# A hybrid decoder layer on one core: the sample group's two score runs and its value sums in one PE run per pair of pages, one raw weight tile, and page turns and gathers at other steps

## The chip, the cores and the metric

The kernel runs on one core of one Trainium2 chip. The metric is the device time of one execution in microseconds (us), and the median of a few executions is compared. Beside these plain times there is one execution taken by the hardware profiler, from which every row quoted below comes. Engine names are those of the profile: PE is the matrix engine's matmuls and PEld its weight loads, DVE the vector engine, ACT the scalar engine, POOL GpSimd, and SP the engine whose queue issues most plain transfers.

## The reference

One decoder layer is computed for a prompt group (1 sequence of 2048 tokens) and for a sample group (8 sequences of 4 new tokens, each with 8192 earlier tokens in a paged cache of keys and values). Both go through the same projection into eleven groups of 512 columns, four mixers (convolution, pooling, stick-breaking attention, cross-attention to 256 memory tokens), gates, an output product and norms. The cut below keeps the projection, the memory product and the stick-breaking attention, which the change touches; the other mixers are as their names say.

```python
D_MODEL, SEQ, DEC_BATCH, DEC_SEQ, PAST_LEN, PAGE_SIZE = 1024, 2048, 8, 4, 8192, 128
SB_HEADS, SB_HEAD_DIM, MEM_HEADS, N_MEM, CONV_K, Q_BLOCK = 8, 64, 4, 256, 31, 128
SPLIT_SIZES = (512,) * 11          # ca cb cg pu pg q k v sg mq mg

def sb_block(q, k, v, bias, q_pos, k_pos):
    z = (jnp.einsum('nqhd,nkhd->nhqk', q, k).astype(jnp.float32) * (SB_HEAD_DIM ** -0.5)
         + bias.astype(jnp.float32)[None, :, None, None])
    mask = (k_pos[None, :] < q_pos[:, None])[None, None]
    log_beta = jax.nn.log_sigmoid(z)
    log_1m = jnp.where(mask, jax.nn.log_sigmoid(-z), 0.0)
    rc = lax.cumsum(log_1m, axis=3, reverse=True)
    a = jnp.exp(jnp.where(mask, log_beta + rc - log_1m, -jnp.inf))
    return jnp.einsum('nhqk,nkhd->nqhd', a.astype(v.dtype), v)

def mem_kv(mem, g, w):
    kv = rms_norm(mem, g) @ w
...

def mixer_layer(x, pos, conv_hist, pool_hist, sb_fn, mk, mv, pre_g, post_g, w_in, ...):
    h = rms_norm(x, pre_g)
    z = h @ w_in
    ca, cb, cg, pu, pg, q, k, v, sg, mq, mg = jnp.split(z, ...)
    y_c, conv_new = conv_branch(ca, cb, conv_hist, w_dw, b_dw, ln_g, ln_b, w_pw, b_pw)
    y_p, pool_new = pool_branch(pu, pool_hist, pos, pool_w, pool_scale)
    y_s = sb_fn(q, k, v, sb_bias).reshape(n, l, W_SB)
    y_m = mem_attend(mq.reshape(n, l, MEM_HEADS, MEM_HEAD_DIM), mk, mv).reshape(n, l, W_MEM)
    mix = jnp.concatenate([y_c * jax.nn.silu(cg), y_p * jax.nn.silu(pg),
                           y_s * jax.nn.silu(sg), y_m * jax.nn.silu(mg)], axis=-1)
    out = rms_norm(mix @ w_out, post_g)
    return x + out, conv_new, pool_new, k, v

# prompt group: sb_fn goes over its own 2048 keys in blocks of Q_BLOCK queries
# sample group: the keys are those of the cache, then its own four
k_past = cache_k[0][page_table].reshape(8, 8192, 8, 64)
v_past = cache_v[0][page_table].reshape(8, 8192, 8, 64)
y_s = sb_block(q, jnp.concatenate([k_past, k], axis=1),
               jnp.concatenate([v_past, v], axis=1), bias, pos_s, k_pos_s)
```

Outputs are both groups' results, the new keys and values, the last rows of convolution and pooling, and the memory keys and values. All is float32.

## The kernel before

**Order of work.** The kernel is one function written in a tile framework. PE's program order is the order of the code (a manual schedule for that engine). For the other engines a scheduler decides the order of the queue, and inserts the waits. Pools hand out tiles by a tag with a number of buffers; a tile of the tag can be written again when the last reader of the buffer's former content is done.

**Stages.** From 0 to about 1490 us the projection z = h @ w_in runs in two parts (1056 and 1024 tokens; column blocks of 384, 384, 288 and of 512, 512), with the product of the 256 memory tokens put between the first groups of part 0, and with convolution, pooling and cross-attention work beside it. The sample group's attention over the cache is interleaved with the projection's matmuls. From about 1490 to 2000 us follows the prompt's stick-breaking attention, then the output product and the norms to 2426.

**Projection weights.** A weight is 1024×128 float32 (512 KB), held as 128×8×128. `load_w` (L222) takes a raw tile "wr" with WR = 2 buffers and issues the load on SP's queue (L226). `split_w` (L229) makes two float32r tiles of it: hi, by ACT's cast (L232), and lo, by POOL's subtraction raw − hi (L233); "whi" and "wlo" have two buffers each. `mm3` (L236) multiplies with 24 matmuls: hi·xhi, hi·xlo, lo·xhi for each of 8 slices (L242). `fill_w` (L745) keeps up to two split weights and as many raw ones as WR allows. The order of the first weights is q0, q1, q2, mem0, mem1, mem2, q3, mem3, mem4, mem5, k0, mem6, mem7, k1, k2, k3, v0; "mem" are the eight weights of the memory product, each used for one block of 256 tokens, while a weight of the projection is used for all column blocks of its part. A group of the projection holds one weight or two (the names tell: z0mq, z0sg).

**Sample group.** The 64 pages of each of 8 sequences are handled in N = 64 steps, called pairs: two pages of four sequences at a time (two groups of 32 pairs). For each page, `load_k` gathers a key tile "kt" (128×2048, 1 MB; POOL issues an indirect DMA, L892), `turn` (L920) lays it into a tile "T" by two DVE transposes of 32×32 blocks (L925) and asks for the key tile of the next pair, and `scores` (L930) does 32 small matmuls into "sSA" (L938; the profile calls their shape 128*32). `load_v` gathers four value tiles "vt" (512 KB each). `weights` (L942) makes the attention weights of a pair: two ACT sigmoids, a DVE scan that goes on from the pair before (L955), a DVE product (L958). `transposes` (L961) turns them on PE and ACT copies them to "saT". `values` (L970) adds the pair's weighted values into "sO" with 16 matmuls (L977). `sample_setup` holds constants: the weights W of the scores, a small mask tile h8x, two tiles sgam.

The generator `sample_stages` is advanced one `yield` at a time by the projection's loop: at each unit of projection work `due` grows by a fixed rate times its cost, and whenever it is above 1 one step is run (L1803), so that the sample group's steps are spread over the projection. There are four steps per pair, and each puts what it holds between two units of projection matmuls:

- A: scores of page 0, then the turn of page 1
- B: transposes of the pair before
- C: scores of page 1, values of the pair before, all four value gathers, weights of this pair, the turn of page 0 of the next pair
- D: nothing

The tags and their buffers: "T" one (TB = 1, 8 KB per partition), "kt" two, "vt" four, "saT" two, "sbe" two.

Of the kernel before, what the change touches and what calls it, by code (L numbers as in the profile page):

```python
# [8 lines left out]
F32 = mybir.dt.float32  # L9
# [9 lines left out]
P = 128  # L19
# [13 lines left out]
PART = 1024  # L33
COLS = (((0, 384), (384, 768), (768, 1056)), ((0, 512), (512, 1024)))
XW = 1056
TB = 1
SMALL = 4
K4 = 4
PACE = 4.0
# [14 lines left out]
VB = 4  # L54
# [4 lines left out]
SEND = 0.97  # L59
XA = 3  # L60
KT = 2
WR = 2


class Tasks:
# [21 lines left out]
def kernel(  # L87
# [9 lines left out]
    pe, act, dve, pool, sp = nc.tensor, nc.scalar, nc.vector, nc.gpsimd, nc.sync  # L97
# [151 lines left out]
    st = zx.enter_context(tc.tile_pool(name="st", bufs=2, side="left"))  # L249
    tasks = Tasks()  # L250

    def big(name, bufs=BIG):
        return st.tile([P, 1088], F32, tag="big", name=name, bufs=bufs)

    def small(name):
        return st.tile([P, 512], F32, tag="small", name=name, bufs=SMALL)
# [488 lines left out]
    def fill_w(n=2):  # L745

        while len(wsplit) < n and (raw or SEQ_W):
# [3 lines left out]
            wsplit[it] = split_w(raw.pop(it), "%d%s%d" % it)  # L751
        while n == 2 and len(raw) < WR and SEQ_W:
            next_raw()
# [53 lines left out]
    def sample_setup(sm, S):  # L807

        ptb = sm.tile([P, NB, NPAGE], I32, tag="T", name="ptb", bufs=TB)
        sp.dma_start(ptb.rearrange("p b n -> p (b n)"), page_table.rearrange("b n -> (b n)").partition_broadcast(P))  # L810
# [55 lines left out]
                    dve.tensor_copy(W[pr, r, :, r, :, i], qv[pr, r, :, t0 : t0 + TS])  # L866
            S["W"].append(W.rearrange("p r j x q i -> p (r j) (x q i)"))

        h8 = sm.tile([P, 4, 2, 4], F32, name="h8x", bufs=1)
        pool.memset(h8, 1.0)  # L870
        pool.affine_select(out=h8, in_=h8, compare_op=ALU.is_ge, fill=0.0, base=0, pattern=[[-32, 4], [-4, 2], [-8, 4]],
                           channel_multiplier=1)
# [5 lines left out]
            dve.tensor_tensor(out=H8, in0=H8, in1=h8[:, i], op=ALU.add)  # L878
        S["H8"] = H8
        S["gam"] = []  # L880
        for k in range(2):
            g = sm.tile([P, 257], F32, name=f"sgam{k}", bufs=1)
            pool.memset(g[:, 256:257], 1.0)
            S["gam"].append(g)
        S["Oc"] = con.tile([P, 2, DH], F32, name="Oc")
        yield

# [6 lines left out]
    def sample_stages(sm, sps, S):  # L894
# [4 lines left out]
        N = 2 * NCK  # L899
        kts, vts, Ts, sSs, As, aTs = {}, {}, {}, {}, {}, {}  # L900
# [8 lines left out]
                gather(kt, krows, S["idk"][:, n // NCK, page(n, ml) : page(n, ml) + 1])  # L909
                kts[n, ml] = kt.rearrange("p (s j d) -> p s j d", s=4, d=32)  # L910

        def load_v(n):
            if n < N:
                vts[n] = []
                for i in range(4):
                    vt = sm.tile([P, 2 * 512], F32, tag="vt", name=f"vt{n}_{i}", bufs=VB)
                    gather(vt, vrows, S["idv"][:, 4 * (n // NCK) + i, page(n, 0) // 2 : page(n, 0) // 2 + 1])
                    vts[n].append(vt)

        def turn(n, ml):  # L920
            if n < N:
                T = sm.tile([P, 4, 16, 32], F32, tag="T", name=f"T{n}_{ml}", bufs=TB)
                kt = kts.pop((n, ml))
                for hh in range(2):
                    dve.transpose(T[:, 2 * hh : 2 * hh + 2].rearrange("p s j t -> p (s j t)"),  # L925
                                  kt[:, 2 * hh : 2 * hh + 2].rearrange("p s j d -> p (s j d)"))
                Ts[n, ml] = T
                load_k(n + 1, ml)
# [12 lines left out]

        def weights(n):  # L942
            sS = sSs.pop(n)
            be = sm.tile([P, 256], F32, tag="sbe", name=f"sbe{n}", bufs=2)
            ga = S["gam"][n % 2]

            tok = sS[:, :256].rearrange("p (m s t) -> p m t s", m=2, s=4)
            by = dict(m=2, s=4)
            act.activation(out=ga[:, 0:256].rearrange("p (m t s) -> p m t s", **by), in_=tok, func=AF.Sigmoid,
                           bias=S["nb1"][:, 0:1], scale=-1.0)  # L950
            act.activation(out=be.rearrange("p (m t s) -> p m t s", **by), in_=tok, func=AF.Sigmoid,
                           bias=S["b1"][:, 0:1])
            E = sm.tile([P, 257], F32, tag="sE", name=f"sE{n}", bufs=2)
            prev = S.get("E") if n % NCK else None
            dve.tensor_tensor_scan(out=E[:, ::-1], data0=ga[:, ::-1], data1=zeros.to_broadcast([P, 257]),  # L955
                                   initial=1.0 if prev is None else prev[:, 0:1], op0=ALU.mult, op1=ALU.max)
            S["E"] = E
            dve.tensor_tensor(out=be, in0=be, in1=E[:, 1:257], op=ALU.mult)  # L958
            As[n] = be

        def transposes(n):  # L961
            aps = S["ps"][:, 256:512]
            bs = As.pop(n).rearrange("p (k s) -> p s k", s=2)
            for k in range(2):
                pe.transpose(aps[:, P * k : P * (k + 1)], bs[:, k, :], ident)
            aT = sm.tile([P, 2, P], F32, tag="saT", name=f"saT{n}", bufs=2)
            act.copy(aT.rearrange("p l r -> p (l r)"), aps)
            aTs[n] = aT.rearrange("p l (x i) -> p l x i", i=4)

# [21 lines left out]
        for _ in range(Y0):  # L991
            yield
        turn(0, 0)
        for n in range(N):
            yield
            scores(n, 0)
            turn(n, 1)
            yield
            if n:
                transposes(n - 1)  # L1000
                yield

            scores(n, 1)
            if n:
                values(n - 1)
                load_v(n)
            weights(n)
            turn(n + 1, 0)
            yield
        yield  # L1010
        yield
        yield
        transposes(N - 1)
        yield
        yield
        values(N - 1)

# [759 lines left out]
    S = {}  # L1777
# [222 lines left out]
    for n, x in enumerate(parts):  # L2000
# [8 lines left out]
        prod, i, h = x  # L2009
# [5 lines left out]
        for k, p_ in enumerate(out_part(x) if n >= len(lead_) else lead if not n else ()):  # L2015
# [5 lines left out]
            if not n:  # L2021

                k, at_ = p_ % 4, p_ // 4
# [41 lines left out]
```

## Time and profile before

| what | value |
|---|---|
| time before, median of 3 runs | 2421.16 us (2418.48 to 2427.0) |
| profiled execution's span | 2426.4 us |
| mean granted clock of PE | 0.982 |
| HBM read / written | 469.28 MB / 90.68 MB, 231 GB/s over the span |
| key gathers: 128 issues, POOL busy | 125.6 us, 981 ns each |
| value gathers: 256 issues, POOL busy | 250.4 us, 978 ns each |
| page turns on DVE: 256 | 308.8 us, 1226 ns each |
| score matmuls: 4096, PE busy | 140.8 us |
| value matmuls: 1024, PE busy | 123.7 us |

Busy times are the time in which an engine has an instruction in work, over the whole span; a matmul's record overlaps the next one's, so for matmuls the distance between starts tells more than the duration. A row of the timeline gives the start, the duration, the engine, the line, the operation, output and inputs; the part in brackets is the idle time of the engine just before, and what ended it. Rows that begin with an engine and a tile and hold "<-" without a time are sums of waits: us in total, times, the longest.

### The profile page before, as it was taken

To read this page: it belongs to the slowest core of one execution; us is meant where nothing else is said; L and a number is where in the kernel's file an instruction comes from. 1 tells how busy PE (TensorE), PEld (TensorE's weight loads), DVE (VectorE), ACT (ScalarE), POOL (GpSimd) and SP (SyncE) were. 2 spreads that over 40 slices of the span, in tenths; PEclk is the share of its full clock that TensorE was granted. 3 is DMA by queue.
4 is the path that set the end of the run, shared out by engine and by line. 5 is a ranking of instruction groups with operands and counts; after the bars stand their busy time and mean duration, and the time that the engine had idled before them with its cause. 6 is when DMAs were issued, how large, how long until landed. Compare 5 with 4: busy or idle time off the path is not lost. (4 is left out here: it accounts for less than half of the span.)

```text
span 2426.4 us, 42151 instructions
## 1 busy us (share of the span) xinstructions
PE 2290.7 (94%) x15962; PEld 1776.1 (73%) x15962; DVE 1736.2 (72%) x2434; ACT 1118.5 (46%) x1939; POOL 1272.7 (52%) x1309
## 2 busy tenths in 40 slices
PE   6999999999999999999999999899999998989997
PEld 6998888898887777777777776455555556777775
DVE  5332784969756665477877877888898857886898
ACT  5322343242442322124241425688989955543444
POOL 2554545556574455655555554576876844433330
PEclk9999999999999999999999999999999999999998
DMA  5678988887778799987877776834332227887764
GB/s 184 213 253 285 350 290 292 290 263 265 261 253 275 271 346 329 312 285 253 290 265 271 260 239 164 239 81 118 101 88 73 63 63 239 272 279 254 238 240 161
DMA packets 340438, 562.15 MB, mean 232 GB/s; under 512 B 28481, under 2 KB 212929, under 8 KB 323834
## 3 DMA queue, kind: packets, MB, share of 16 engines
q1 hardware_dynamic: 284858, 290.72, 39.1%
q0 software_dynamic: 55376, 268.72, 31.1%
q8 instruction: 126, 2.06, 0.3%
q14 instruction: 78, 0.64, 0.1%
HBM read 469.28 MB, written 90.68 MB: 231 GB/s over the span
## 5 line engine op out<-in xcount | busy, mean ns | idle before, releaser
L925 DVE STREAM_TRANSPOSE T<-kt 128x1024 f32<-128x1024 f32 x256 | 308.8, 1226 | 193.6 <-PE sSA L938 183.0
L892 POOL DMA_INDIRECT vt<-in_cache_v_dram,idv x256 | 250.4, 978 | 239.7 <-PE sO L977 178.8
L583 DVE SCALAR_TENSOR_TENSOR cacc<-U,par,cacc 128x512 f32<-128x512 f32 x480 | 360.1, 750 | 11.8
L1277 POOL TENSOR_TENSOR be<-be,E 128x512 f32<-128x512 f32 (+2 forms) x320 | 303.5, 956 | 117.0 <-DVE E L1268 52.6
L1268 DVE TENSOR_TENSOR_SCAN E<-gam,cr,ZM 128x513 f32<-128x513 f32 x192 | 232.9, 1262 | 14.4 <-ACT gam L1253 13.2
L892 POOL DMA_INDIRECT kt<-in_cache_k_dram,idk x128 | 125.6, 981 | 206.9 <-DVE T L925 152.5
L1288 PEld LDWEIGHTS AT<-ident,be 128*128 128x128 f32 x1088 | 117.9, 142 | 127.3 <-ACT at L1294 45.3
L1885 PE MATMUL acc<-wohi,mh 128*128 128x512 f32 (+1 forms) x480 | 193.6, 403 | 3.9 <-DVE mh L1650 2.0
L1253 ACT ACTIVATE gam<-S,nbias_bc 128x1024 f32<-128x1024 f32 (+1 forms) x160 | 172.5, 1078 | 51.2 <-ACT be L1255 18.9
L1885 PE MATMUL acc<-wolo,mh 128*128 128x512 f32 (+1 forms) x480 | 190.8, 397 | 0.0
L1885 PE MATMUL acc<-wohi,ml 128*128 128x512 f32 x448 | 179.2, 400 | 12.1 <-DVE ml L1650 12.1
L1248 PE MATMUL S<-kT,Q 128*128 128x512 f32 (+1 forms) x640 | 177.9, 401 | 6.1 <-ACT be L1255 2.6
L1288 PE MATMUL AT<-ident,be 128*128 128x128 f32 x1088 | 158.4, 284 | 13.8 <-DVE at L1292 3.9
L1255 ACT ACTIVATE be<-S,bias_bc 128x1024 f32<-128x1024 f32 (+1 forms) x160 | 171.4, 1071 | 0.0
L1304 PE MATMUL av<-at,V 128*64 128x512 f32 (+3 forms) x640 | 153.0, 557 | 1.7 <-DVE sbo L1309 1.7
L938 PE MATMUL sSA<-T,W 128*32 128x128 f32 x4096 | 140.8, 277 | 7.6 <-DVE T L925 6.4
L938 PEld LDWEIGHTS sSA<-T,W 128*32 128x32 f32 x4096 | 105.4, 110 | 44.9 <-issue 37.2
L977 PE MATMUL sO<-vt,saT 128*32 128x512 f32 x1024 | 123.7, 597 | 0.0
L1248 PEld LDWEIGHTS S<-kT,Q 128*128 128x128 f32 x640 | 107.3, 196 | 22.2 <-ACT be L1255 3.5
L1650 DVE TENSOR_TENSOR ml<-mr,mh 128x512 fp32r<-128x512 f32 x108 | 97.0, 905 | 33.6 <-ACT mh L1639 33.4
L1265 DVE TENSOR_TENSOR_SCAN E<-gam,ZM 128x128 f32<-128x128 f32 (+3 forms) x128 | 96.4, 802 | 29.3 <-ACT gam L1253 22.3
L1294 ACT COPY at<-AT 128x512 f32<-128x512 f32 x192 | 109.0, 656 | 14.4 <-PE AT L1288 14.4
(571 smaller groups left out, 6032.8 us busy)
## 6 DMA issues: line engine op xcount, KB each, us to landing
Q<-qd SPq DMA_DIRECT2D x64, 256.0 KB
mr<-mixd SPq DMA_DIRECT2D x32, 512.0 KB
mr<-mixd SPq DMA_DIRECT2D x48, 256.0 KB
wor<-in_w_out_dram SPq DMA_DIRECT2D x20, 512.0 KB
xtp<-in_x_prompt_dram SPq DMA_DIRECT2D x16, 512.0 KB
kT<-kd SPq DMA_DIRECT2D x64, 128.0 KB
wor<-in_w_out_dram SPq DMA_DIRECT2D x32, 256.0 KB
msd<-mr SPq DMA_DIRECT2D x32, 256.0 KB
```

What stands on the lines that cost most here:

```text
L583: dve.scalar_tensor_tensor(out=ps, in0=U[:, a + k : a + k + H], scalar=wd[:, k : k + 1], in1=ps, op0=ALU.mult, op1=ALU.add)
L892: pool.indirect_dma_start(out=dst, out_offset=None, in_=rows, in_offset=bass.IndirectOffsetOnAxis(ap=idx, axis=0))
L925: dve.transpose(T[:, 2 * hh : 2 * hh + 2].rearrange("p s j t -> p (s j t)"), kt[:, 2 * hh : 2 * hh + 2].rearrange("p s j d -> p (s j d)"))
L938: pe.matmul(sSs[n][32 * g : 32 * g + 32, P * ml : P * (ml + 1)], lhsT=W[:, jj, :], rhs=T[:, :, jj, :], start=i == 0, stop=i == 3, tile_pos ...
L1248: pe.matmul(S[:, j, :w], lhsT=Q[hh][:, x, P * (q2 + j) : P * (q2 + j + 1)], rhs=KT[hp, hh, kc][:, :w], start=x == 0, stop=x == 1)
L1253: act.activation(out=ga[:, :, 512 - w : 512], in_=S[:, :, :w], func=AF.Sigmoid, bias=nbias_bc[:, h : h + 1], scale=-1.0)
L1255: act.activation(out=be[:, :, :w], in_=S[:, :, :w], func=AF.Sigmoid, bias=bias_bc[:, h : h + 1])
L1268: dve.tensor_tensor_scan(out=E[:, j][:, ::-1], data0=ga[:, j][:, ::-1], data1=ZM[:, 0:1].to_broadcast([P, 513]), initial=carry[hh, q2][:, ...
L1277: pool.tensor_tensor(out=be[:, j, :m], in0=be[:, j, :m], in1=E[:, j, 513 - w : 513 - w + m], op=ALU.mult)
L1288: pe.transpose(ap_[:, P * qt : P * (qt + 1)], A[hp, qb, kc, hh, qt][:, P * r : P * (r + 1)], ident)
L1304: pe.matmul(av[64 * hh : 64 * hh + 64, c], lhsT=V[:, 4 * kc + r, 64 * hh : 64 * hh + 64], rhs=ats.pop((hp, qb, kc, r, hh))[:, c], start=dg ...
L1885: pe.matmul(o[:rows], lhsT=m[a][:, k, :rows], rhs=W[prod, 4 * h + k][w], start=not cont and h == k == n == 0, stop=h == 1 and k == 3 and n ...
```

## The change

- A pair's scores of both pages and the value sums of the pair before become one step (A), and so one run on PE. The transposes of the pair's own weights come two steps later, in the same pair (C). Steps B and C take one page turn of the next pair each; step D holds nothing. The value gathers are written in two halves, two in A behind the value sums, two in B.
- Two T tiles in place of one; ahead of the first pair both its pages are turned, and two steps pass. At the end the last value sums come one step after the last pair.
- One raw weight tile in place of two. The tile "big" shrinks from 1088 to 1056 columns; h8x takes a buffer of the tag "vt"; sgam, sbe and saT have one buffer in place of two.

The arithmetic and the number of matmuls, turns, gathers and loads stay the same.

```diff
--- before.py
+++ after.py
@@ -33,7 +33,7 @@
 PART = 1024
 COLS = (((0, 384), (384, 768), (768, 1056)), ((0, 512), (512, 1024)))
 XW = 1056
-TB = 1
+TB = 2
 SMALL = 4
 K4 = 4
 PACE = 4.0
@@ -59,7 +59,7 @@
 SEND = 0.97
 XA = 3
 KT = 2
-WR = 2
+WR = 1
 
 
 class Tasks:
@@ -250,7 +250,7 @@
     tasks = Tasks()
 
     def big(name, bufs=BIG):
-        return st.tile([P, 1088], F32, tag="big", name=name, bufs=bufs)
+        return st.tile([P, 1056], F32, tag="big", name=name, bufs=bufs)
 
     def small(name):
         return st.tile([P, 512], F32, tag="small", name=name, bufs=SMALL)
@@ -866,7 +866,7 @@
                     dve.tensor_copy(W[pr, r, :, r, :, i], qv[pr, r, :, t0 : t0 + TS])
             S["W"].append(W.rearrange("p r j x q i -> p (r j) (x q i)"))
 
-        h8 = sm.tile([P, 4, 2, 4], F32, name="h8x", bufs=1)
+        h8 = sm.tile([P, 4, 2, 4], F32, tag="vt", name="h8x", bufs=VB)
         pool.memset(h8, 1.0)
         pool.affine_select(out=h8, in_=h8, compare_op=ALU.is_ge, fill=0.0, base=0, pattern=[[-32, 4], [-4, 2], [-8, 4]],
                            channel_multiplier=1)
@@ -878,10 +878,9 @@
             dve.tensor_tensor(out=H8, in0=H8, in1=h8[:, i], op=ALU.add)
         S["H8"] = H8
         S["gam"] = []
-        for k in range(2):
-            g = sm.tile([P, 257], F32, name=f"sgam{k}", bufs=1)
-            pool.memset(g[:, 256:257], 1.0)
-            S["gam"].append(g)
+        g = sm.tile([P, 257], F32, name="sgam", bufs=1)
+        pool.memset(g[:, 256:257], 1.0)
+        S["gam"].append(g)
         S["Oc"] = con.tile([P, 2, DH], F32, name="Oc")
         yield
 
@@ -909,10 +908,10 @@
                 gather(kt, krows, S["idk"][:, n // NCK, page(n, ml) : page(n, ml) + 1])
                 kts[n, ml] = kt.rearrange("p (s j d) -> p s j d", s=4, d=32)
 
-        def load_v(n):
+        def load_v(n, some=range(4)):
             if n < N:
-                vts[n] = []
-                for i in range(4):
+                vts.setdefault(n, [])
+                for i in some:
                     vt = sm.tile([P, 2 * 512], F32, tag="vt", name=f"vt{n}_{i}", bufs=VB)
                     gather(vt, vrows, S["idv"][:, 4 * (n // NCK) + i, page(n, 0) // 2 : page(n, 0) // 2 + 1])
                     vts[n].append(vt)
@@ -941,8 +940,8 @@
 
         def weights(n):
             sS = sSs.pop(n)
-            be = sm.tile([P, 256], F32, tag="sbe", name=f"sbe{n}", bufs=2)
-            ga = S["gam"][n % 2]
+            be = sm.tile([P, 256], F32, tag="sbe", name=f"sbe{n}", bufs=1)
+            ga = S["gam"][0]
 
             tok = sS[:, :256].rearrange("p (m s t) -> p m t s", m=2, s=4)
             by = dict(m=2, s=4)
@@ -963,7 +962,7 @@
             bs = As.pop(n).rearrange("p (k s) -> p s k", s=2)
             for k in range(2):
                 pe.transpose(aps[:, P * k : P * (k + 1)], bs[:, k, :], ident)
-            aT = sm.tile([P, 2, P], F32, tag="saT", name=f"saT{n}", bufs=2)
+            aT = sm.tile([P, 2, P], F32, tag="saT", name=f"saT{n}", bufs=1)
             act.copy(aT.rearrange("p l r -> p (l r)"), aps)
             aTs[n] = aT.rearrange("p l (x i) -> p l x i", i=4)
 
@@ -991,27 +990,25 @@
         for _ in range(Y0):
             yield
         turn(0, 0)
+        turn(0, 1)
+        yield
+        yield
         for n in range(N):
-            yield
             scores(n, 0)
-            turn(n, 1)
-            yield
-            if n:
-                transposes(n - 1)
-                yield
-
             scores(n, 1)
             if n:
                 values(n - 1)
-                load_v(n)
+                load_v(n, (0, 1))
             weights(n)
+            yield
             turn(n + 1, 0)
-            yield
-        yield
-        yield
-        yield
-        transposes(N - 1)
-        yield
+            if n:
+                load_v(n, (2, 3))
+            yield
+            transposes(n)
+            turn(n + 1, 1)
+            yield
+            yield
         yield
         values(N - 1)
 
```

## The prediction

> **What bounds the kernel now.** I read the span and the page's sums first, then the busy slices, then the windows of the stages that the change touches.
>
> ```profile
> core 0: 2426.4 us, clock 0.982
> PE 2290.7 (94%) x15962; PEld 1776.1 (73%) x15962; DVE 1736.2 (72%) x2434; ACT 1118.5 (46%) x1939; POOL 1272.7 (52%) x1309
> PE   6999999999999999999999999899999998989997
> PEclk9999999999999999999999999999999999999998
> 60.00:120.00 60.00, 57.44 (x414) 55.93 (x414) 21.26 (x36) 18.79 (x34) 33.49 (x24) 1.00 0.68 208
> 160.00:1490.00 1330.00, 1304.21 (x10710) 1062.22 (x10710) 903.88 (x1201) 435.85 (x815) 718.91 (x658) 0.99 0.81 278
> 900.00:1000.00 100.00, 100.00 (x790) 74.93 (x789) 51.93 (x63) 24.20 (x43) 55.66 (x45) 1.00 0.97 336
> ```
>
> A row of windows gives the stretch, its length, the busy time and instructions of PE, PEld, DVE, ACT and POOL, then clock, DMA share and GB/s. PE is busy for 1304 of the 1330 us in which the sample pairs run, and all of 900 to 1000. So there the time is what PE has to do: an edit gains only what it takes off PE, and costs only where it makes PE wait. At 60 to 120, where weights follow each other fastest, PE is 96% busy with one raw tile spare. In 900 to 1000 the DMA engines are at 0.97 too, so PE work saved there may not all become time.
>
> **One run for scores and value sums.** Score matmuls have another tile shape than the projection's, and going over and back costs time.
>
> ```profile
> 633.81 0.34 PE L242 MATMUL z0mq<-xlo,whi0mq 128*128 128x384 f32 x1
> 633.98 0.34 PE L242 MATMUL z0mq<-xhi,wlo0mq 128*128 128x384 f32 x1
> 634.25 1.08 PE L938 MATMUL sSA<-T,W 128*32 128x128 f32 x32
> 635.54 0.34 PE L242 MATMUL z0sg<-xlo,whi0sg 128*128 128x384 f32 x1
> L938 PE MATMUL sSA<-T,W x4096: 269/273/423, 168.5 to 1455.7; 128*32 128x128 f32 x196
> L977 PE MATMUL sO<-vt,saT x1024: 592/592/1061, 193.9 to 1484.7; 128*32 128x512 f32 x171
> ```
>
> Projection matmuls start 633.98 − 633.81 = 0.17 us apart. Between those at 633.98 and 635.54 lie 1.56 us, with the 32 score matmuls and one projection matmul that the view leaves out (at 635.26), so the scores displace 1.56 − 2 × 0.175 = 1.21 us. Their own pitch is (1.08 − 0.27)/31 = 0.026, so 32 cost 0.83, and 1.21 − 0.83 = 0.38 us is the price of one excursion. Scores of the first page now join the run that scores of the second and value sums already shared: three runs per pair become two, in 63 pairs: **−23.6 us**. Bounds −20 (DMA share 0.97) and −24.
>
> **One raw weight tile.** Before, a load waits for the split (ACT's cast, then POOL's subtraction) of the weight two earlier, so it lands while the last one is split. Now it waits for the weight just before, and load, cast and subtraction stand in a row.
>
> ```profile
> 57.28 2.40 POOL L233 TENSOR_TENSOR wlo0q<-wr0q,whi0q 128x1024 fp32r<-128x1024 f32 x1 [5.72 <-ACT whi0q L232]
> 98.75 2.39 POOL L233 TENSOR_TENSOR wlo0mem<-wr0mem,whi0mem 128x1024 fp32r<-128x1024 f32 x1 [1.76 <-ACT whi0mem L232]
> 101.17 0.37 SPq L226 DMA_DIRECT2D wr0mem<-in_w_mem_kv_dram  x1
> 106.23 1.04 ACT L232 CAST whi0mem<-wr0mem 128x1024 fp32r<-128x1024 f32 x1 [3.92 <-DMA wr0mem<-in_w_mem_kv_dram]
> 107.36 2.39 POOL L233 TENSOR_TENSOR wlo0mem<-wr0mem,whi0mem 128x1024 fp32r<-128x1024 f32 x1 [1.74 <-ACT whi0mem L232]
> 121.47 2.40 POOL L233 TENSOR_TENSOR wlo0k<-wr0k,whi0k 128x1024 fp32r<-128x1024 f32 x1 [1.76 <-ACT whi0k L232]
> 125.73 0.42 PE L242 MATMUL z0k<-xhi,whi0k 128*128 128x384 f32 x1
> ```
>
> The load at 101.17 is issued right behind the subtraction that frees its tile (98.75 + 2.39 = 101.14), and the cast at 106.23 had waited 3.92 us for its data alone: load 106.23 − 101.17 = 5.06, cast and subtraction 107.36 + 2.39 − 106.23 = 3.52, handover 0.03. The cycle becomes 8.61 us a weight. From the subtraction of q2 (57.28) to that of k1 (121.47) lie 11 steps, the eight memory weights among them: 64.2 us before, 11 × 8.61 = 94.7 then, +30.5. The last one was ready at 121.47 + 2.40 = 123.87 and first used at 125.73, a slack of 1.86: **+28.7 us**. PE has nothing to fill these waits, since the sample's first scores come at 168.5.
>
> The load's price is the large unknown. From both sides:
>
> ```profile
> 0.83 0.39 SPq L301 DMA_DIRECT2D xtp<-in_x_prompt_dram  x1
> 4.71 1.06 ACT L195 ACTIVATE sq<-xtp 128x1024 bf16<-128x1024 f32 x1 [2.39 <-DMA xtp<-in_x_prompt_dram]
> 1.74 0.43 SPq L226 DMA_DIRECT2D wr0q<-in_w_in_dram  x1
> 9.04 1.05 ACT L232 CAST whi0q<-wr0q 128x1024 fp32r<-128x1024 f32 x1 [2.85 <-DMA wr0q<-in_w_in_dram]
> ```
>
> 512 KB of x alone on empty queues takes 4.71 − 0.83 = 3.88 us: cycle 7.43, +15.7. A weight behind other loads takes 9.04 − 1.74 = 7.30: cycle 10.85, +53.3. I take 5.06, the same kind of load in the same stage.
>
> The Trainium skill, "DMA: Bandwidth & Descriptors", section "Anatomy of one DMA — SWDGE (gpsimd) path", fits a DMA issued from GpSimd as 2.0 us plus its bytes over 436 GB/s, an estimate of 3.2 us for 512 KB. By it the cycle would be 6.75 and the front stage +8.2 instead of +28.7. This load, issued by SP and with a row of 512 bytes per descriptor, took 5.06 in the trace.
>
> **Half clock after a wait.** A long wait of PE has a second price here.
>
> ```profile
> 365.60:369.03 3.43, 0.00 (x0) 0.00 (x0) 0.12 (x1) 2.58 (x6) 0.09 (x1) 1.00 1.01 408
> 369.03:375.86 6.83, 6.12 (x49) 5.44 (x50) 5.43 (x11) 1.85 (x3) 1.82 (x2) 0.50 0.57 235
> ```
>
> After 3.43 us without a matmul the granted clock is 0.50 for 6.83 us, 3.4 us lost. In the front stage two blocks take two weights in turn and leave PE empty for some 6 us. Part of the lost clock falls where PE would wait for the next weight anyway: **+3 us** (0 to 10).
>
> **Weights further on.** A weight there serves 24 matmuls in each of three or two column blocks, some 3 × 24 × 0.17 = 12 us, and the sample's runs beside them; that is above the cycle of 8.61, so the single tile is hidden. Only where a group takes two weights at once is the second late, against
>
> ```profile
> PE z0sg L242 <- POOL wlo0sg L233: 2.2, 2, 2.0
> 25.69 0.67 PE L242 MATMUL z0q<-xhi,whi0q 128*128 128x384 f32 x1
> ```
>
> 2.2 us for such waits now: **+3 us** (0 to 6). At the start, q1's load moves behind q0's split, to 9.04 + 1.05 + 2.4 = 12.5, and is split by 12.5 + 8.6 = 21, before the first projection at 25.69: nothing; without that cover it would be the difference.
>
> **Gathers.** Before, the gathers stand on POOL's queue as value rows, then keys:
>
> ```profile
> 874.01 0.95 POOL L892 DMA_INDIRECT vt<-in_cache_v_dram,idv  x1 [3.90 <-PE sO L977]
> 879.03 0.93 POOL L892 DMA_INDIRECT kt<-in_cache_k_dram,idk  x1 [0.31 <-issue]
> 871.86 1.90 PE L977 MATMUL sO<-vt,saT 128*32 128x512 f32 x16
> 890.99 1.47 PE L977 MATMUL sO<-vt,saT 128*32 128x512 f32 x12
> 808.24 1.24 DVE L925 STREAM_TRANSPOSE T<-kt 128x1024 f32<-128x1024 f32 x1
> 811.17 0.45 DVE L958 TENSOR_TENSOR sbe<-sbe,sE 128x256 f32<-128x256 f32 x1
> PE sSA L938 <- DVE T L925: 6.4, 4, 3.8
> q0 software_dynamic: 55376, 268.72, 31.1%
> ```
>
> Four gathers and the step to the next take (879.03 − 874.01)/4 = 1.25 us each. The edit writes the last two value gathers a step later, but in the built program's queue order a key gather comes first and the four value gathers follow nearly together. It waits for the two turns of its page (DVE's queue takes them straight after the scores), so the last value gather is issued 2 × 1.24 + 1.25 + 4 × 1.25 = 8.7 us after the scores, some 5 us later than now; queued behind it on POOL are only the second key gather and the next weight's subtraction, which has slack. Landing takes 5.06 to 7.30 more (the loads above): 14 to 16 us. The sums that need it come one pair later, 20.5 us in the mean ((1484.7 − 193.9)/63), 890.99 − 871.86 = 19.1 in the dense stretch. Of that period the gathers alone hold all DMA engines for 0.311 × 2426.4/64 = 11.8 us, so a landing can drag: I take **+8 us** (0 to 40), a short wait in a few pairs.
>
> In return the second T tile lets the turns run a step ahead. PE's waits for T, 6.4 us in four, the longest as long as the gap that halved the clock above, mostly vanish: **−5 us** (−8 to 0). Weights to transposes is two steps instead of three, about 10 us; DVE's chain takes 811.17 + 0.45 − 808.24 = 3.4, so that stays hidden, and a wait there would show if the chain stood behind both pages' turns (another 5 us, still inside). The single copies of sgam, sbe and saT and h8x in a shared tile bind nothing that wasn't already in order; the smaller tile "big" only makes room: nothing.
>
> **Sum:** 28.7 + 3 + 3 + 8 − 23.6 − 5 = **+14.1 us**, 2426.4 → 2440.5 in the profile's terms. The profiled execution's time is its span, 5.2 above the median of the runs, 2421.16; so 2421.2 + 14.1 ≈ **2435 us**.
>
> **The rivals.** *Short loads.* With the queues emptier because each load goes alone, a load lands in 3.88 us; nothing is late further on, no wait halves the clock, and the merge pays in full: 15.7 − 23.6 − 8 = −15.9, **2405 us**. For it: the DMA share of 0.68 at 60 to 120. Against it: that share holds the very loads, and 101.17 to 106.23 was already one weight alone. (By the skill's fit it would be 8.2 in place of 15.7, 2398.)
>
> *The gathers don't spread.* This is the case in which the change doesn't do what it says, and slower than my forecast: value rows land last, and set the pair's length. It decides from a landing of 19.1 − 8.7 = 10.4 us after the last issue. At 1.5 us in half of the pairs, 32 × 1.5 = 48 in place of 8: **2475 us**. For it: DMA at 0.97 where the gathers' 11.8 us is most of the pair. Against it: a total of 336 GB/s there carries all of it today, and no more bytes move.
>
> *Front and merge cancel.* The load lies between (4.4 us, cycle 7.95, +21.4), later costs are absent: 21.4 − 23.6 = −2, **2419 to 2421 us**, no change. For it: 4.4 is as near to 3.88 as to 5.06, and transposes of memory rows may fill some of the waits. Against it: it needs every smaller cost to be nothing.
>
> **How the numbers follow.** Forecast 0.50, with its own range 2424 to 2446 (the half clock, group and gather terms at both ends); short loads 0.20; gathers 0.12; cancel 0.18. A change of 0.3% is 7.3 us, about what this measurement can tell from none (the three runs spread over 8.5). Faster is the rival at 2405: 0.20, and some of the cancelling case: 0.22. Same: the rest of that case and the forecast's low end: 0.20. Slower: 0.58. The range goes down to 2402 (most of the short loads) and up to 2460, leaving out most of the gathers' case and the load's bound of 7.30: some 0.2 of the chance.
>
> **What would show it.** In the front: casts of the memory weights that wait for DMA each time, subtractions 8.6 us apart, PE waiting for wlo by some 25 to 30 us between 57 and 155, and memory blocks ending late by that much. In the pairs: two runs of 128*32 matmuls per pair, and the stretch from the first scores to the last value sums shorter by about 20 us with PE still near full. On POOL, a key gather ahead of four value gathers. I am wrong if subtractions follow at 7.5 us or less, if PE waits for value rows by more than 10 us in all, or if half-clock windows multiply behind the front.

## The result, and the profile after

The changed kernel takes 2467.98 us in the median of four runs (2460.88 to 2472.16), the kernel before 2422.01: a ratio of 1.0175, 95% interval 1.0155 to 1.0196, so **46 us slower** where 14 were forecast. Slower was the likeliest case, but the time lies above the range (2460). The profiled execution is the fastest of the four, that of before the slowest of its own, so that the two traces differ by 32.8 us only. Reading them apart therefore shows two thirds of the loss; the other part is in the runs' spread and is settled by timed comparisons further down.

These are the page's and the windows' rows of after that answer to the first ones of before.

```profile
core 0: 2459.2 us, clock 0.976
PE 2292.7 (93%) x15962; PEld 1795.0 (73%) x15962; DVE 1734.0 (71%) x2434; ACT 1113.2 (45%) x1935; POOL 1284.4 (52%) x1308
PE   6879998999999899999999999899999998999897
PEclk9989999999999999999999999899999998999998
60.00:120.00 60.00, 48.81 (x307) 45.79 (x307) 19.52 (x30) 13.70 (x24) 25.52 (x18) 0.91 0.44 140
900.00:1000.00 100.00, 99.54 (x771) 76.01 (x770) 57.97 (x71) 27.36 (x50) 53.32 (x42) 1.00 0.97 334
```

In the first slices PE and its clock fall below 9, and 60 to 120 holds 307 matmuls where before there were 414. The dense stretch at 900 looks as it did. How late the front ends is read from the first matmul of v0 (the start given first, of before, then of after):

```profile
L242 PE MATMUL z0v<-xhi,whi0v x96: 288/337/445, 173.1 to 237.9; 128*128 128x384 f32 x64, 128*128 128x288 f32 x32
```

```profile
L242 PE MATMUL z0v<-xhi,whi0v x96: 288/337/443, 206.1 to 270.3; 128*128 128x384 f32 x64, 128*128 128x288 f32 x32
```

So the whole difference between the traces, 33.0 us, is there at 206 us, before the first pair. From there to the last projection weight both take the same, 1320.6 and 1321.9 us (windows of before, then of after):

```profile
173.10:1493.70 1320.60, 1294.81 (x10617) 1052.63 (x10616) 902.08 (x1201) 432.67 (x807) 712.77 (x653) 0.99 0.82 278
```

```profile
206.10:1528.00 1321.90, 1288.22 (x10649) 1065.26 (x10649) 897.74 (x1201) 427.15 (x803) 720.85 (x652) 0.99 0.80 278
```

The single raw tile cost what was forecast for the front. The merged run, forecast at −23.6, shows up as 6.6 us less busy time of PE and 7.9 us more idle time, and as nothing in the length.

**The front, row by row.** The subtractions of the eight memory weights, before and after: count, durations, first and last start.

```profile
L233 POOL TENSOR_TENSOR wlo0mem<-wr0mem,whi0mem x8: 2373/2389/2527, 60.8 to 114.0; 128x1024 fp32r<-128x1024 f32 x8
```

```profile
L233 POOL TENSOR_TENSOR wlo0mem<-wr0mem,whi0mem x8: 2345/2382/2392, 67.6 to 141.6; 128x1024 fp32r<-128x1024 f32 x8
103.67 0.38 SPq L226 DMA_DIRECT2D wr0mem<-in_w_mem_kv_dram  x1
107.99 1.05 ACT L232 CAST whi0mem<-wr0mem 128x1024 fp32r<-128x1024 f32 x1 [0.66 <-DMA wr0mem<-in_w_mem_kv_dram]
109.12 2.38 POOL L233 TENSOR_TENSOR wlo0mem<-wr0mem,whi0mem 128x1024 fp32r<-128x1024 f32 x1 [4.17 <-ACT whi0mem L232]
59.74 2.40 POOL L233 TENSOR_TENSOR wlo0q<-wr0q,whi0q 128x1024 fp32r<-128x1024 f32 x1 [5.73 <-ACT whi0q L232]
149.54 2.38 POOL L233 TENSOR_TENSOR wlo0k<-wr0k,whi0k 128x1024 fp32r<-128x1024 f32 x1 [3.77 <-ACT whi0k L232]
153.01 0.42 PE L242 MATMUL z0k<-xhi,whi0k 128*128 128x384 f32 x1
```

From mem0 to mem7 are nine steps (q3 and k0 among them): (141.6 − 67.6)/9 = 8.22 us each, against (114.0 − 60.8)/9 = 5.91 before; forecast was 8.61. The load took 107.99 − 103.67 = 4.32 us where I had taken 5.06. The Trainium skill's "DMA: Bandwidth & Descriptors", section "Anatomy of one DMA — SWDGE (gpsimd) path", gives the estimate of 3.2 us that the prediction names; the load measured here is above it. The last three rows are the subtractions of q2 and of k1 and k1's first matmul, which comes 153.01 − 125.73 = 27.3 us later than before.

The rest of the 33 us stands at the end of the front, where nothing was forecast (before, then after):

```profile
143.06 1.25 DVE L925 STREAM_TRANSPOSE T<-kt 128x1024 f32<-128x1024 f32 x1 [5.79 <-DMA kt<-in_cache_k_dram,idk]
144.40 4.55 PE L855 MATMUL qps<-qsT,rep 128*128 128x32 f32 x32 [1.09 <-DVE b L845]
```

```profile
173.17 2.37 DVE L924 STREAM_TRANSPOSE T<-kt 128x1024 f32<-128x1024 f32 x2 [6.87 <-DMA kt<-in_cache_k_dram,idk]
175.47 0.12 DVE L845 COPY b<-bps 128x1 f32<-128x1 f32 x1
175.64 1.70 PE L855 MATMUL qps<-qsT,rep 128*128 128x32 f32 x7 [5.08 <-DVE b L845]
172.87:186.52 13.65, 10.88 (x45) 10.78 (x46) 8.80 (x24) 0.00 (x0) 8.04 (x8) 0.50 0.80 291
```

In both kernels DVE's queue holds the first page's turn ahead of a small copy of the sample's setup, so the copy waits for the page's keys, and PE for the copy. PE's wait was 1.09 us and is now 5.08; the clock is 0.50 for 13.65 us, from 172.87 on and so from within the wait, where it was for 6.83 us before (from 147.16). The kernel before with one raw tile (e2 below) waits 4.47 us here, so the longer wait comes with the raw tile and not with the second T tile.

**The merged run.** It is as short as it was meant to be (timeline of after; the run stands between two projection matmuls):

```profile
1077.24 0.40 PE L242 MATMUL z1pu<-xhi,wlo1pu 128*128 128x512 f32 x1
1077.57 1.95 PE L937 MATMUL sSA<-T,W 128*32 128x128 f32 x64
1079.34 1.90 PE L976 MATMUL sO<-vt,saT 128*32 128x512 f32 x16
1081.50 0.39 PE L242 MATMUL z1cg<-xlo,whi1cg 128*128 128x512 f32 x1
```

1081.50 − 1077.24 less two pitches of 0.23 is 3.80 us (one projection matmul, at 1081.17, is left out of the view); the same reckoning over all undisturbed runs gives medians of 1.21 and 2.93 before and 3.80 after, a saving of 0.34 a pair, 21 us in 63. In return there are rows that before did not have:

```profile
929.74 1.03 PE L976 MATMUL sO<-vt,saT 128*32 128x512 f32 x6
931.24 1.93 PE L976 MATMUL sO<-vt,saT 128*32 128x512 f32 x10 [0.46 <-DMA vt<-in_cache_v_dram,idv]
PE sO L976 <- DMA vt<-in_cache_v_dram,idv: 5.1, 6, 2.8
DVE T L924 <- DMA kt<-in_cache_k_dram,idk: 26.7, 10, 6.9
```

A value sum stops in the middle for its rows; summed over the distances between starts, eight pairs lose 12.9 us so. DVE's waits for keys are 26.7 us where they were 6.6. Most of these come with the second T tile and not with the merged run, since e3 below, in the old order with two T tiles, has 22.4.

Why PE's busy time fell by 6.6 us and not by 21 can be estimated from the same trace. Of the 12.9 us only 5.1 are idle time; the other 7.8 lie within matmuls that count as busy. And from v0's first matmul to the last projection weight the granted clock is 0.50 for 30.7 us in six windows, before for 17.1 in three, which is up to 6.8 us of slower matmuls. 6.6 + 7.8 + 6.8 is about the 21.

### The profile page after: what moved, and what is told of

The parts are those of the page before. It is cut to its first block, busy times and chain, and to the rows that moved or that the text cites. A ratio compares the mean times of both kernels' runs of the same rounds, so it can differ in the third digit from the quotient of the medians.

```text
span 2459.2 us, 42020 instructions
## 1 busy us (share of the span) xinstructions
PE 2292.7 (93%) x15962; PEld 1795.0 (73%) x15962; DVE 1734.0 (71%) x2434; ACT 1113.2 (45%) x1935; POOL 1284.4 (52%) x1308
## 5 line engine op out<-in xcount | busy, mean ns | idle before, releaser
L1265 DVE TENSOR_TENSOR_SCAN E<-gam,cr,ZM 128x513 f32<-128x513 f32 x192 | 232.9, 1262 | 13.9 <-ACT gam L1250 12.7
L891 POOL DMA_INDIRECT kt<-in_cache_k_dram,idk x128 | 130.8, 1022 | 198.2 <-DVE T L924 147.6
L976 PE MATMUL sO<-vt,saT 128*32 128x512 f32 x1024 | 134.1, 598 | 5.2 <-DMA vt<-in_cache_v_dram,idv 5.1
L937 PE MATMUL sSA<-T,W 128*32 128x128 f32 x4096 | 125.6, 275 | 0.0
```

The source lines that it names most:

```text
L891: pool.indirect_dma_start(out=dst, out_offset=None, in_=rows, in_offset=bass.IndirectOffsetOnAxis(ap=idx, axis=0))
L937: pe.matmul(sSs[n][32 * g : 32 * g + 32, P * ml : P * (ml + 1)], lhsT=W[:, jj, :], rhs=T[:, :, jj, :], start=i == 0, stop=i == 3, tile_pos ...
L1265: dve.tensor_tensor_scan(out=E[:, j][:, ::-1], data0=ga[:, j][:, ::-1], data1=ZM[:, 0:1].to_broadcast([P, 513]), initial=carry[hh, q2][:, ...
```

## Experiments

Two questions: is the loss the single raw tile, and where does the merged run's saving go? Ratios are to the kernel before in the same comparison; 1% is 24 us.

**e1: a second raw tile for the front alone.**

```diff
-        raw_ = wp.tile([P, ND, P], F32, tag="wr", name="wr%d%s%d" % it, bufs=WR)
+        n = X["nw"] = X.get("nw", -1) + 1
+        if n % 2 and n <= 13:
+            raw_ = X["mp"].tile([P, ND, P], F32, tag="wr", name="wr%d%s%d" % it, bufs=1)
+        else:
+            raw_ = wp.tile([P, ND, P], F32, tag="wr", name="wr%d%s%d" % it, bufs=WR)
...
-        while n == 2 and len(raw) < WR and SEQ_W:
+        while n == 2 and len(raw) < (2 if X["nw"] < 13 else WR) and SEQ_W:
...
```

> The changed kernel with a second raw tile for the first fourteen weights alone (every second one of them lies in the pool of the memory stage, which ends before the sample pairs begin); from the fifteenth weight on there is one raw tile, and the pairs are as changed. Theory 1: the front stage holds +33 us of the +46 (the matmul that opens v0's first block starts at 206.1 after against 173.1 before), and the pairs come out even, since what the single PE run saves is given back there. Then this kernel is 26 to 33 us faster than the changed one: 2435 to 2442 beside 2422, and v0 opens at 174 to 180. Rival: the front's wait is absorbed further on, the pairs are what the change made slower (gathers, later weights): then it stays above 2455.

2435.2 us, 1.0055 (1.0037 to 1.0073): 33 us less than the changed kernel by the medians, 29 by the ratios, and v0 opens at 174.3. The front's share stands.

**e2: the kernel before with one raw tile** (`WR = 1`, nothing else).

> The kernel before with one raw weight tile and nothing else changed. Theory 1: load, cast and subtraction in a row cost 25 to 28 us up to k1, some more in the clock after the waits, and 0 to 5 us where a group takes two weights: 2450 to 2458 beside 2422. Rival (the raw tile is hidden but for a few waits, and the front was late for the smaller 'big' tiles or the turned pages): under 2435.

2463.8 us, **1.0175 (1.0152 to 1.0197)**, the ratio of the whole change. The tile alone costs 43 us, more than the theory's 28 to 36; all else in the change comes out near zero.

**e5: the kernel before with one raw tile from the fifteenth weight on** (e1's edit on before).

> The kernel before with one raw tile from the fifteenth weight on, and two for the first fourteen (as in e1): the later part of the single tile alone. One raw tile throughout cost the kernel before 43 us (2463.8 against 2420.8), and giving the front its second tile took 33 us off the changed kernel. If front and later part add up, this is 2421 + 10 = 2428 to 2434. If the later weights are hidden (the prediction's +3), 2421 to 2425; then the front cost 40 and the changed kernel without it should have been at 2428 rather than 2435.

2431.9 us, 1.0028 (1.0007 to 1.0048): 6.7 us for the later weights, with an interval from 2 to 12. With e1's 29 to 33 for the front that is near e2's 43.

**e3: e1 with the pairs in the order of before.**

```diff
...
+            yield
             scores(n, 0)
+            turn(n, 1)
+            yield
+            if n:
+                transposes(n - 1)
+                yield
             scores(n, 1)
             if n:
                 values(n - 1)
-                load_v(n, (0, 1))
+                load_v(n)
             weights(n)
-            yield
             turn(n + 1, 0)
-            if n:
-                load_v(n, (2, 3))
-            yield
-            transposes(n)
-            turn(n + 1, 1)
-            yield
             yield
...
```

> e1 with the pairs in the order of before: scores of page 0, transposes of the pair before, then scores of page 1 with the value sums, all four value gathers at once; two T tiles, one raw tile from the fifteenth weight on, and the single sgam, sbe and saT stay. Theory 1: a pair's third run costs 0.34 us again (displaced time 1.21 and 2.93 against 3.80 us of the merged run), 63 times, +21, but the waits for value rows (12.9 us) and for half clock go: within 10 us of e1, 2415 to 2430. Rival (the merge pays in full and the loss in the pairs is the one raw tile's): 12 to 24 us slower than e1.

2437.1 us, 1.0077 (1.0055 to 1.0098). The new order is 2 us faster than the old one by the medians, 5 by the ratios (the intervals overlap), not the rival's 12 to 24; the level is 7 above what the theory expected.

**e4: value gathers ahead of the keys.**

```diff
-                load_k(n + 1, ml)
+                with tc.issue_after(S["lastv"].ins):
+                    load_k(n + 1, ml)
...
-                load_v(n, (0, 1))
+                load_v(n)
...
```

> e1 with all four value gathers written behind the value sums, and on POOL's queue each key gather held behind the value gathers of the pair, so that value rows are asked for some 5 us earlier. Theory 1: the value sums' waits (12.9 us in eight pairs of the changed kernel) and the half clock behind the longest go: 10 to 18 us faster than e1, 2420 to 2430 or less, with T late by no more than 3 us in all. Rival (DMA is what is full: a landing moved forward moves the keys back by the same, and PE waits for T instead): within 5 us of e1.

2448.3 us, 1.0113 (1.0096 to 1.0129): **13 us slower than e1**, where 10 to 18 faster were expected. The waits in the trace of e4:

```profile
DVE T L930 <- DMA kt<-in_cache_k_dram,idk: 68.2, 18, 13.9
PE my L505 <- ACT pT L520: 12.0, 3, 6.1
PE ms L479 <- DVE mh0mq L716: 9.1, 2, 6.1
```

PE's waits for value rows all but vanish, but DVE now waits 68 us for keys (25 in e1), and work of the cross-attention that PE needs is queued behind. That is the rival's mechanism with a larger price than it had, and with PE waiting for the cross-attention rather than for T: moved forward, one gather moves the other back.

**n1 and n2: no gathers after the first pair**, in the new order (on e1) and the old (on e3); key and value tiles of the first pair are used throughout.

```diff
-                kt = sm.tile([P, 4 * 512], F32, tag="kt", name=f"kt{n}_{ml}", bufs=KT)
-                gather(kt, krows, S["idk"][:, n // NCK, page(n, ml) : page(n, ml) + 1])
+                if n == 0:
+                    S["kt", ml] = sm.tile([P, 4 * 512], F32, tag="kt", name=f"kt{n}_{ml}", bufs=KT)
+                    gather(S["kt", ml], krows, S["idk"][:, n // NCK, page(n, ml) : page(n, ml) + 1])
+                kt = S["kt", ml]
...
```

> e1 without the gathers of all pairs but the first: every pair turns and multiplies the first pair's key and value tiles, so matmuls, turns, sigmoids and scans stay and the output is another. Read with n2. Theory 1: what the merged run saves is given back by gathers that come late (PE's waits for value rows, DVE's for key rows with PE's work queued behind them). Without gathers it then pays in full: n1 is 18 to 25 us faster than n2. Rival: it is given back by DVE's and ACT's order (turns of both pages ahead of the mixers' work), whatever the gathers do: n1 within 8 us of n2.

> e3 (pairs in the order of before, two T tiles) without the gathers of all pairs but the first, output as n1's another. The PE waits of e3 for gathers are few (one wait for value rows, about 1.7 us), so the gathers' absence should take off only what the DMA queues and DVE's 22 us of waits for keys cost: 2415 to 2432 by both theories; n1 against n2 decides.

2394.2 (0.9862, 0.9837 to 0.9887) and 2405.8 us (0.9907, 0.9882 to 0.9932): the new order gains 11.6 us, between both theories (all runs of n1 lie below 2396, all of n2 above 2404). The windows from v0's first matmul to the last projection weight, n1 and then n2:

```profile
175.30:1461.80 1286.50, 1268.47 (x10649) 1058.08 (x10649) 898.46 (x1201) 427.89 (x803) 341.60 (x276) 0.99 0.26 82
```

```profile
172.80:1473.20 1300.40, 1286.28 (x10618) 1049.97 (x10616) 897.39 (x1199) 433.24 (x807) 343.36 (x276) 1.00 0.26 81
```

PE is busy 17.8 us less, and 13.9 of it reach the length; 3.9 go into idle time. Against the 2 to 5 us that the order gains with gathers, these take 7 to 10 of the 21; the rest isn't theirs.

**n3 and n4: without the key gathers alone, without the value gathers alone** (one half of n1's edit each).

> e1 without the key gathers of all pairs but the first (the first pair's key tiles are turned again each time, so the output is another); the value gathers stay. All gathers together cost the new order 41 us (2435 to 2394) and the old one 31. If it is bytes on the DMA queues that count, half the bytes are gone: about 2415. If it is value rows landing late behind a key gather, the value waits of 12 to 15 us go, and DVE's waits for keys (25 us) with them, though some would have been hidden: 2398 to 2408.

> e1 without the value gathers of all pairs but the first (the first pair's value rows are used again, output another); the key gathers stay. Bytes alone: about 2415. If the keys hold up DVE's queue and PE's work stands behind that: 2418 to 2428, above the kernel without key gathers; if PE's own waits for value rows are the larger part: 2400 to 2412, below it or equal.

2416.0 (0.9949, 0.9932 to 0.9966) and 2409.3 us (0.9924, 0.9905 to 0.9943). By the ratios e1 loses 1.06% without keys, 1.31% without value rows, and 1.93% without both: each half alone brings more than half of the whole. n3 came out where bytes alone were expected (2415), n4 in the range expected if PE's own waits for value rows are the larger part. So neither kind of gather is the cause by itself; the nearest reading is that both crowd the same queues at one time. These two were not run in the old order, so they show what the gathers cost this kernel and not what each takes from the merge.

**w_k43, o_k43 and b_k43: two raw tiles throughout, the room from the tag k4** (`WR = 2`, `K4 = 3`): the change, the change in the old order, and the kernel before with `K4 = 3` alone.

> The changed kernel with two raw weight tiles throughout; the room comes from one 4 KB tile of the tag k4 (three in place of four: rows on their way out and x rows of part 1). Theory 1: the front's 33 us and the later weights' some 10 go: 2468 - 43 = 2425, less or more by what the lost k4 tile costs; 2415 to 2435. Rival (the pairs lose by the new order itself): 2435 or more.

> w_k43 with the pairs in the order of before: two raw tiles, two T tiles, three k4 tiles, single sgam, sbe and saT. w_k43 was 7.9 us above the kernel before, e3 (old order) 2 us above e1. If the new order pays nothing net and the loss lies in the second T tile and what goes with it (DVE takes up turns whose keys have not landed, 22 us of such waits in e3 against 7 before), this is 5 to 13 us above the kernel before. Rival (the new order of the pairs is what costs): within 4 us of the kernel before.

> The kernel before with three k4 tiles in place of four, the control for w_k43 and o_k43. If the fourth tile is not needed: within 3 us of the kernel before, and the +7.9 of w_k43 is order and T tiles. If it is above 5 us, that much of w_k43 is the missing tile.

1.0033 (1.0014 to 1.0053), 1.0047 (1.0030 to 1.0063) and 1.0043 (1.0025 to 1.0061). The control itself lost 10 us, so k4 was no free room; against it the change is 2.5 us faster and the old order with a second T tile equal, by ratios whose intervals overlap.

**w_big4 and b_big4: the same with the room from the tag big** (`WR = 2`, `BIG = 4`; the kernel before with `BIG = 4`).

> The changed kernel with two raw tiles throughout, the room taken from one of five 'big' tiles. To be read against b_big4 as w_k43 against b_k43: the order of the pairs and the second T tile alone, -5 to +5 us if the merged run's saving is given back, -15 to -25 if it is kept and the k4 tile only hid it.

> The kernel before with four 'big' tiles in place of five, the control for w_big4. Nothing known of it in the traces: 0 to +25 us, since the convolution's and pooling's rows lie in these tiles.

2428.1 us, **0.9992 (0.9978 to 1.0006)**, and 2427.6, 1.0008 (0.9993 to 1.0023), beside 2430.6 of before. Here the control is free, and the change without its single raw tile is no different from the kernel before: against its control 4 us less by the ratios, 0.5 more by the medians. The saving isn't kept. Windows as above, the control and then w_big4:

```profile
171.70:1491.80 1320.10, 1294.57 (x10617) 1053.07 (x10616) 903.88 (x1201) 432.66 (x807) 712.54 (x653) 0.99 0.82 279
```

```profile
174.90:1495.80 1320.90, 1282.82 (x10649) 1061.63 (x10648) 898.27 (x1201) 428.33 (x803) 719.64 (x652) 0.99 0.79 278
```

PE is busy 11.7 us less, and the stage is 0.8 longer: idle time grew from 25.5 to 38.1 us. The longest of PE's waits, which grew by 4.2 of these 12.6 us, shows how gathers can fill it (timeline of the control: POOL's gathers, an SP store, DVE, PE):

```profile
348.06 0.98 POOL L892 DMA_INDIRECT kt<-in_cache_k_dram,idk  x1 [4.26 <-DVE T L925]
357.26 1.00 POOL L892 DMA_INDIRECT vt<-in_cache_v_dram,idv  x1 [0.16 <-issue]
359.88 0.33 SPq L411 DMA_DIRECT2D mkTd<-mkbT  x1
366.82 0.69 DVE L517 TENSOR_TENSOR pL<-mpt,pT 128x512 fp32r<-128x512 f32 x1 [5.28 <-DMA mkTd<-mkbT]
367.66 0.98 PE L475 MATMUL ms<-mkT,mh0mq 128*128 128x256 f32 x3 [4.57 <-DVE pL L517]
```

and of w_big4:

```profile
357.48 1.01 POOL L891 DMA_INDIRECT kt<-in_cache_k_dram,idk  x1 [3.13 <-DVE sm L485]
359.93 1.00 POOL L891 DMA_INDIRECT vt<-in_cache_v_dram,idv  x1 [0.17 <-issue]
360.76 0.32 SPq L411 DMA_DIRECT2D mkTd<-mkbT  x1
364.96 0.94 POOL L891 DMA_INDIRECT kt<-in_cache_k_dram,idk  x1 [0.30 <-issue]
373.65 0.69 DVE L517 TENSOR_TENSOR pL<-mpt,pT 128x512 fp32r<-128x512 f32 x1 [9.56 <-DMA mkTd<-mkbT]
374.49 0.98 PE L475 MATMUL ms<-mkT,mh0mq 128*128 128x256 f32 x3 [8.81 <-DVE pL L517]
```

In the control one key gather leaves 9 us ahead of the other five; in the new order all six (both key pages and four value tiles) leave within 7.5 us. The store of mkTd, issued among them, holds its buffer for 373.65 − 360.76 = 12.9 us instead of 6.9; DVE waits for that buffer, and PE for DVE: 8.8 us idle in place of 4.6. The Trainium skill's "DMA: Bandwidth & Descriptors", section "Queues, rings and completion order", says that a DMA engine takes the queues with work in turn; that a store stretches when more gathers are in flight agrees with it.

This is one example and no proof for the order. Without gathers the wait is gone in both orders (n1 and n2), so it needs the gathers. But it is 4.4 us in the kernel before and in the changed kernel alike, 8.6 in e1, and 9.8 in h2, which has the old order; what sets its length in each run is not shown. In w_big4 a 512 KB load (mkb) also leaves just before the store, at 359.12, in the control at 355.06; no run separates that load from the key gather.

**h1 and h2: the raw tile in two halves**, on the changed kernel and on the kernel before (the same 4 KB; h2 has no whole second tile).

```diff
+        for h in range(2):
+            raw_.append(wp.tile([P, ND // 2, P], F32, tag="wr", name="wr%d%s%d" % it, bufs=2))
+            wq.dma_start(raw_[-1], sv[:, 4 * h : 4 * h + 4])
...
+        for h in range(2):
+            hs = slice(4 * h, 4 * h + 4)
+            act.copy(hi[:, hs], raw[h])
+            pool.tensor_tensor(out=lo[:, hs], in0=raw[h], in1=hi[:, hs].bitcast(F32), op=ALU.subtract)
```

> The changed kernel with its one raw weight tile cut into two halves of 256 KB (the same 4 KB per partition): each half is loaded, cast and subtracted by itself, so a half's load runs while the other half is split. If the single tile's cost is the load that can't start before the whole split ends, a weight's cycle in the front falls from 8.16 us (measured) to about half load 4 + half split 1.8 = 5.8, the 5.84 that the front took before: the front's 33 us go, 2468 to 2430 or 2440. If the cost is the load's own fixed time (it doesn't fall with size and two stand in a row): above 2455.

> The kernel before with its two raw tiles replaced by the two halves of one (4 KB per partition less). By the first reading of h1: within 8 us of the kernel before. h1 minus this one is then the order of the pairs with its second T tile: by the runs with three k4 tiles (w_k43 against b_k43, 2438.8 and 2433.5 beside kernels before of 2428 and 2426) between -5 and +5 us; by the prediction's sum -20.

2449.9 us, 1.0089 (1.0056 to 1.0122), and 2441.4, 1.0050 (1.0033 to 1.0068). With the same memory the loss falls from 46 to 22 us in the changed kernel and from 43 (e2) to 12 in the kernel before, less than expected: v0 opens at 183.3 in h1, 9 us after e1. So the row of load and split is a large part of the cost, and a half load takes more than half of the whole one's time (h1):

```profile
87.11 0.37 SPq L229 DMA_DIRECT2D wr0mem<-in_w_mem_kv_dram  x1
89.92 0.62 ACT L237 CAST whi0mem<-wr0mem 128x512 fp32r<-128x512 f32 x1 [1.84 <-DMA wr0mem<-in_w_mem_kv_dram]
```

That is 2.81 us for 256 KB where the whole took 4.32. Other casts of h1's front end a wait for PE to leave the hi tile, so the load isn't all that is left. By the medians the new order is 9 us slower than the old here, outside the −5 to +5 expected; the intervals overlap.

## Why the prediction went wrong, step by step

- **The front: right in mechanism, near in size in part by luck.** Up to k1's first matmul 27.3 us were measured for +28.7. The eleven steps cost less than taken, (149.54 − 59.74)/11 = 8.16 us each for 8.61, so +25.6 for +30.5; but q2 was already 2.5 us late (59.74 for 57.28), which had been put at nothing. The other 5.7 of the 33.0 was unforeseen: the longer wait for the setup's copy, 4.0, and the half clock with it. The +3 for the clock had been meant for the waits between the memory weights.
- **The later weights: too small.** +3 (0 to 6), measured 6.7 by e5, with an interval of 2 to 12.
- **The merge: this step failed.** The saving itself was near (0.34 for 0.38 a pair, 21 for 23.6). What failed is the sentence on which it rested, that in a stage busy for 1304 of 1330 us an edit gains what it takes off PE, and the small bounds (−20 to −24) that followed. The runs show PE's busy time falling by less and its idle time rising by as much as it falls: w_big4 0.9992 where the sum of these steps (−23.6 + 8 − 5 = −20.6) gives 0.9915. Without gathers 11.6 us arrive. With them it is 2 to 5 by the ratios in three comparisons (e1 to e3, w_k43 and w_big4 to their controls), and −9 in the fourth (h1 to h2), and in all four the intervals overlap. That the gathers take some 7 to 10 us of the 21 rests on n1 and n2; through which transfers is argued.
- **The gathers: right in mechanism, too small in reach.** 12.9 us of PE's own waits for value rows for +8. The prediction had the order on POOL, a key gather, four value gathers nearly together and the second key gather. It gave no price to what else waits while they are under way: other stages' transfers, and DVE's queue behind a turn. Two of its own signs for being wrong came true here: over 10 us of waits for value rows, and more half-clock windows behind the front (six for three). The rival of the gathers named the place, and priced it wholly in value rows (48 us), which isn't what happened.
- **The waits for T: right.** PE's are gone (−6.4), and DVE's waits for keys stand in their place (26.7 for 6.6 us), with the mixers' work behind.
- **The range.** It took the bounds of the raw tile's price alone for the upper end, and the merge as sure. With the merge at zero the same sum is 2421 + 28.7 + 3 + 3 + 0 = 2456, and with e5's price some 2460. The raw tile's three terms, 34.7 in all, were 43 in e2; with the 20.6 of the merge's steps that did not arrive this makes up 29 of the 32 us between the forecast +14 and the measured +46.

Open: without gathers 9 of the 21 us are still missing. n1's trace has 3.9 us more idle time than n2's and some more half clock, and its v0 opens 2.5 us later; what causes these was not tried. The second T tile, with what goes with it, costs 12 us by the ratios in the old order beside one raw tile (e3 against e5) and nothing beside two (o_k43 against b_k43); why was not tried either. No version that computes everything is measurably faster than the kernel before.

## What to carry to other kernels

Before taking a buffer away, line up what it lets overlap (here a load under the split of the last weight) and look for the stage with the shortest period: a tile that is idle in most of a kernel can carry its front. Joining two steps of one engine also joins the times at which their buffers come free; ask which transfers then leave together, and who else waits in those queues. That an engine is busy for 1304 of 1330 us is no proof that its work is all that bounds the stage, since some of its waits can count as busy: take the transfers out in one run, and see whether the length follows.

## What the runs showed of the hardware beyond that

The clock lost beside one wait weighed as much as the wait: around PE's 5.08 us the granted clock was 0.50 for 13.65 us, in which PE worked for 10.88, so up to 5.4 us were lost. The changed kernel's four runs go with their mean clocks: 2461 and 2464 us at 0.976 and 0.975, 2472 twice at 0.974 and 0.973, and 0.003 of 2470 us is 7 of the 11 between them.
